# The first layer's feed-forward in the form of the last one: context tokens by themselves, latents as seven block products, the down projection summed in PSUM

## The chip, the cores and the metric

The kernel runs on one core of a Trainium2 chip. The core has a matrix engine (TensorE, PE in the profile; its weight loads are PEld), three engines for elementwise work (VectorE or DVE, ScalarE or ACT, GpSimd or POOL), and SyncE (SP), which here only issues transfers. The engines run side by side, each through a list of instructions of its own, in order, and wait for one another on semaphores. Work tiles lie in SBUF; matmuls write to PSUM, which holds eight banks of 128x512 numbers in fp32. The metric is the device time of one execution in microseconds.

## The reference

A trunk of two layers over a stream of 1024 latent tokens and 256 context tokens, 1024 wide. Each layer mixes the tokens (attention beside a state-space scan, one input and one output projection), and then applies a feed-forward that is 2816 wide. Norms stand ahead of and behind both parts, and a modulation computed from `c` (for the context from `c_ctx`) scales, shifts and gates them. The change is in the feed-forward and its surroundings:

```python
def swiglu(h, w_gate, w_up, w_down):
    return (jax.nn.silu(h @ w_gate) * (h @ w_up)) @ w_down

for l in range(DEPTH):                       # DEPTH = 2
    update_ctx = l < DEPTH - 1
    ...
    f_l = rmsnorm(x_lat, norm_ffn_pre[l]) * (1.0 + sc2_l) + sh2_l
    x_lat = x_lat + g2_l * rmsnorm(swiglu(f_l, w_gate[l], w_up[l], w_down[l]), norm_ffn_post[l])
    if update_ctx:
        ...
        f_c = rmsnorm(x_ctx, norm_ffn_pre[l]) * (1.0 + sc2_c) + sh2_c
        x_ctx = x_ctx + g2_c * rmsnorm(swiglu(f_c, w_gate[l], w_up[l], w_down[l]), norm_ffn_post[l])
return x_lat
```

The first layer's feed-forward works on all 1280 tokens, the last one's on the 1024 latents alone.

## The kernel before

**Tokens and numbers.** The tokens are ten tiles of 128: 0 and 1 are context, 2 to 9 latents. The normed, modulated input of a feed-forward is kept transposed in three buffers: `hc` (context, 256 columns), `ha` (tiles 2 to 5, 512 columns), `hb` (tiles 6 to 9). Each operand in fp32 is split into a high part, a cast on ACT (line 113), and a low part, a subtraction (line 114) on VectorE or POOL. A product is three matmuls, high·high, high·low and low·high, by `mm3` (lines 227 to 229).

**Weights.** A weight *unit* is 512 KB. SP issues its load into one of two buffers `raw`; it is cast and subtracted into one of five ring buffers `w_t`, and `free()` gives the slot to the next unit of a list that `plan()` writes. `pump()` (which `free()` calls) chooses the subtracting engine: POOL for most. A scheduler then orders the instructions on each engine by its own estimate of times; generators (`fill`, `step`) put side work between the steps.

**Feed-forward of layer 0** (`ffn`). The 2816 inner columns are 22 blocks `ff` of 128. It runs twice, first over context and tiles 2 to 5, then over tiles 6 to 9. For each block: gate and up for each span (two PSUM banks `ps_w`, eight steps of `mm3` each), silu on ACT, the product with up (line 1167), a split, and then the down projection of the block, tokens by 1024 columns, in banks `ps_s`. Its result is added on VectorE to `ffn_acc` in SBUF (line 1186; line 1184 copies for the first block). All three weight matrices pass twice: 132 units. Between the blocks run the modulation of the coming layer (`mod_stream`, matmuls of line 278; its 512 KB tiles `raw_m` also go through the two `raw` buffers), the scalings and flips of rows for the next span or layer (`pre_scale` line 361, `pre_flip` line 378), and after the last block `finish`, the norm behind the feed-forward (`postnorm`: squares of line 242, `rstd` lines 234 and 235, lines 806 and 812).

**Feed-forward of layer 1** (`ffn_last`). The latents are a 2x2 block form: two spans of tokens by two halves of the 1024 input columns, blocks B11, B12, B21, B22. For each `ff`, gate and up together are the other factor, with blocks A11, A12 (gate) and A21, A22 (up). Seven block products in place of eight, each four steps of `mm3` over 512 columns, give both results; VectorE adds and subtracts them (for example line 1046). Their factors are A11, A12, A22 and sums S1 to S4 of weight blocks (`wblock`), and B11, B21, B22 and sums T1 to T4 of input blocks, made by `quads` (transposes line 989, sums line 1003, splits lines 998 and 999). Since the sums need the last tiles, three *heads* (the two products A11·B11 and A12·B21) run first. The split result `hid` goes to memory. `down_all` reads it back through `hid_ring` and sums all 22 blocks in PSUM, for groups of tiles (2,3,4), (5,6,7), (8,9), each tile two banks; the down weights pass once per group.

Of the kernel before, what the change touches and what calls it, by code (L numbers as in the profile page):

```python
# [54 lines left out]
class Trunk:  # L55
    def __init__(self, nc, tc, es, I, out):
# [36 lines left out]
        self.hf_d = d("hf", [KT // 2, 2, P, 512])  # L93
        self.hid_d = d("hid", [NFF, P, 2, LAT])
# [34 lines left out]
    def plan(self):  # L129
        I = self.I  # L130
        seq = []
# [13 lines left out]
        for l in range(DEPTH):  # L145
# [8 lines left out]
            if l == 1:  # L154
                flat = [(ff, b) for ff in range(3) for b in ("A11", "A12")]
                flat += [(ff, b) for ff in range(3) for b in (("S4",) if ff == 0 else ()) + ("S2", "S3", "S1", "A22") + (("S4",) if ff else ())]
                flat += [(ff, b) for ff in range(3, NFF) for b in ("A11", "A12", "S2", "S3", "S1", "A22", "S4")]
                self.wpos = {b: (i // 2, i % 2) for i, b in enumerate(flat)}
                for i in range(0, len(flat), 2):
                    seq.append(((l, "w", i // 2), flat[i:i + 2], None))  # L160
                for grp in range(len(self.GROUPS)):
                    for ff in range(NFF):
                        seq.append(((l, "d", grp, ff), [(slice(0, 1024), I["w_down"][l][ff * P:(ff + 1) * P, :].unsqueeze(1))], (1, 1024)))
                break
            for grp in range(2):
                order = [("g", 0), ("u", 0), ("d", 0)]
                for ff in range(1, NFF):
                    order += [("g", ff), ("u", ff), ("d", ff)]
                for kind, ff in order:
                    if kind == "d":  # L170
                        seq.append(((l, kind, grp, ff), [(slice(0, 1024), I["w_down"][l][ff * P:(ff + 1) * P, :].unsqueeze(1))], (1, 1024)))
                    else:
                        w = I["w_gate" if kind == "g" else "w_up"][l]
                        seq.append(((l, kind, grp, ff), [(slice(0, P), kp(w, ff * P, (ff + 1) * P))], (KT, P)))
        self.seq, self.nemit, self.freed, self.U, self.ws = seq, 0, set(), {}, {}

    def pump(self):
        while self.nemit < len(self.seq):
# [11 lines left out]
            self.U[key] = self.unit(parts, shape, None, None if key[1] == "z" or i < 4 or key[2:] == (0, 0) or len(key) == 4 and key[:3] == (1, "d", 2) and key[3] % 2 else self.nc.gpsimd)  # L190
# [7 lines left out]
    GROUPS = ((2, 3, 4), (5, 6, 7), (8, 9))  # L198

    def wblock(self, w, ff, name):  # L200
        nc = self.nc
        st = self.ws.setdefault(ff, {})

        def raw(kind):
            if kind not in st:
                st[kind] = self.raw.tile([P, 1024], F32, tag="raw", name="raw_t")
                src = self.I["w_gate" if kind == "g" else "w_up"][1][:, ff * P:(ff + 1) * P].rearrange("(k p) n -> p k n", p=P)
                nc.sync.dma_start(st[kind].rearrange("p (k n) -> p k n", k=KT), src)
            return st[kind]
# [11 lines left out]
        self.split(w[:, 0], w[:, 1], src, nc.gpsimd)  # L221
        if name == ("A22" if ff == 0 else "S4") or name == "A12" and ff < 3:
# [71 lines left out]
    def mod_stream(self, l, secs, ps):  # L294
        for sec in secs:
# [62 lines left out]
    def pre_scale(self, xs):  # L358
        for a in xs:
            r = self.row_rstd([a[:, 0:512], a[:, 512:1024]], D)  # L360
            self.nc.gpsimd.tensor_scalar(a, a, r, 1.0, op0=ALU.mult, op1=ALU.mult)

    def pre_flip(self, xs, span, i, l, which, keep=None):
# [1012 lines left out]
```

## Time and profile before

Three runs took 3284.16, 3285.5 and 3300.47 us, a median of 3285.5. The profiled execution took 3276.44 us, its span (first to last instruction) is 3274.6 us.

| | |
|---|---|
| Profiled execution; span | 3276.44 us; 3274.6 us |
| Mean granted TensorE clock | 0.975 |
| Layer 0's feed-forward, first to last of its matmuls | 840.15 to 1858.40 us |
| Layer 1's products without a hole | 2640 to 3000 us |
| Layer 1's down projection, some of it | 3040 to 3270 us |

A row of a group of instructions gives line, engine, operation, written and read tiles, shape and count, then busy time and the mean of one in ns, then the idle time of the engine just ahead of them and what ended it. A row of a wait gives who waited for whom, then the total in us, the number of times and the longest. A row of a timeline gives the start and duration in us; an x2 there stands for two instructions in a row. In rows of windows each engine has its busy time and count. The time of one matmul in a timeline includes the depth of the pipeline; the distance between starts is what it costs.

### The profile page before, as it was taken

What the parts mean: (1) busy time and instruction counts of PE and PEld (TensorE: products, weight loads), DVE (VectorE), ACT (ScalarE), POOL (GpSimd) and SP (SyncE); (2) the same over time, 40 slices, a digit from 0 to 9 for tenths busy, and PEclk for the clock granted to TensorE, in tenths of its full rate; (3) what the DMA queues carried; (4) which work ended last, traced back from release to release, by engine and by line L of the source; (5) the groups of instructions that cost most, each with busy time, mean ns of one, the idle gap of its engine ahead of it and who ended that gap; (6) DMA issues with size and microseconds to landing.
All of it is one profiled execution on the core that took longest, in us unless ns stands there. A gap on an engine that the chain in (4) does not pass through costs nothing. (4 is left out here: it accounts for less than half of the span.)

```text
span 3274.6 us, 44714 instructions
## 1 busy us (share of the span) xinstructions
PE 3087.7 (94%) x16411; PEld 2558.0 (78%) x16411; DVE 1725.6 (53%) x3190; ACT 1337.0 (41%) x2441; POOL 1557.2 (48%) x1428
## 2 busy tenths in 40 slices
PE   6999889999899999988999999899999699999997
PEld 4777778888777888876777788688888588888885
DVE  2657567765343344436333556769666665654003
ACT  4433357666422112234222344337666533333232
POOL 4236565444433222336334533755444754454653
PEclk8999899999999999999999999999999899999999
DMA  6376553221333321235444415653222433336776
GB/s 226 100 218 219 188 183 103 65 65 65 116 117 104 99 88 59 71 117 167 135 137 134 136 47 158 223 178 104 65 65 79 134 127 106 110 109 207 240 240 205
DMA packets 328267, 434.61 MB, mean 133 GB/s; under 512 B 22440, under 2 KB 237640, under 8 KB 327792
## 3 DMA queue, kind: packets, MB, share of 16 engines
q1 hardware_dynamic: 268160, 341.04, 33.8%
q10 hardware_dynamic: 59888, 90.71, 7.6%
q8 instruction: 130, 2.13, 0.3%
q14 instruction: 89, 0.73, 0.1%
HBM read 340.67 MB, written 91.01 MB: 132 GB/s over the span
## 5 line engine op out<-in xcount | busy, mean ns | idle before, releaser
L114 POOL TENSOR_TENSOR w_t<-raw_t,w_t 128x1024 fp32r<-128x1024 f32 (+2 forms) x353 | 719.1, 2045 | 1020.2 <-ACT w_t L113 1004.6
L113 ACT CAST w_t<-raw_t 128x1024 fp32r<-128x1024 f32 (+2 forms) x380 | 335.1, 891 | 710.4 <-DMA raw_t<-in_w_down 216.5
L1186 DVE TENSOR_TENSOR ffn_acc<-ffn_acc,ps_s 128x512 f32<-128x512 f32 x400 | 270.9, 686 | 199.9 <-PE ps_s L229 198.4
L862 DVE TENSOR_SCALAR_CACHE_REDUCE att_a<-ps_s 128x512 f32<-128x512 f32 (+1 forms) x400 | 227.1, 587 | 136.8 <-PE ps_s L861 128.5
L870 POOL TENSOR_SCALAR att_a<-att_a,att_st 128x1280 f32<-128x1280 f32 (+1 forms) x144 | 183.2, 1275 | 151.0 <-DVE att_st L869 84.2
L1167 DVE TENSOR_TENSOR s2t<-s2t,ps_w 128x256 f32<-128x256 f32 (+1 forms) x66 | 39.5, 598 | 339.6 <-PE ps_w L229 331.7
L227 PE MATMUL ps_w<-ha,w_t 128*128 128x512 f32 x528 | 208.2, 396 | 6.5 <-DVE s2t L1046 5.5
L228 PE MATMUL ps_w<-ha,w_t 128*128 128x512 f32 x528 | 207.9, 394 | 2.5 <-DVE ha L386 2.5
L229 PE MATMUL ps_w<-ha,w_t 128*128 128x512 f32 x528 | 207.2, 393 | 0.0
L113 ACT CAST xt<-s2t 128x512 fp32r<-128x512 f32 (+2 forms) x147 | 79.9, 543 | 299.1 <-DVE s2t L1167 202.9
L883 PE MATMUL ps_w<-cst_all,att_a 128*128 128x128 f32 x1312 | 197.3, 275 | 0.2
L868 ACT ACTIVATE att_a<-att_a,att_st 128x1280 f32<-128x1280 f32 (+1 forms) x144 | 183.2, 1273 | 33.6 <-DVE att_st L867 30.4
L227 PE MATMUL ps_s<-w_t,xt 128*128 128x512 f32 x446 | 179.9, 403 | 10.2 <-ACT xt L113 4.8
L229 PE MATMUL ps_s<-w_t,xt 128*128 128x512 f32 x446 | 174.9, 395 | 1.5 <-DVE xt L114 1.5
L228 PE MATMUL ps_s<-w_t,xt 128*128 128x512 f32 x446 | 175.7, 394 | 0.0
L114 DVE TENSOR_TENSOR xt<-s2t,xt 128x512 fp32r<-128x512 f32 (+2 forms) x147 | 143.5, 977 | 43.1 <-ACT xt L113 41.6
L883 PEld LDWEIGHTS ps_w<-cst_all,att_a 128*128 128x128 f32 x1312 | 152.8, 141 | 11.0 <-DVE xt L806 5.5
L464 DVE SCALAR_TENSOR_TENSOR xt<-row,convw,xt 128x512 f32<-128x512 f32 (+1 forms) x128 | 123.3, 1017 | 70.0 <-ACT xt L462 52.4
L227 PE MATMUL ps_w<-hb,w_t 128*128 128x512 f32 x352 | 142.3, 404 | 1.1 <-ACT s2t L381 1.1
L228 PE MATMUL ps_w<-hb,w_t 128*128 128x512 f32 x352 | 141.1, 401 | 0.0
L229 PE MATMUL ps_w<-hb,w_t 128*128 128x512 f32 x352 | 140.5, 399 | 0.0
L227 PEld LDWEIGHTS ps_w<-ha,w_t 128*128 128x128 f32 x528 | 100.6, 191 | 28.2 <-DVE s2t L1046 5.7
(355 smaller groups left out, 8405.8 us busy)
## 6 DMA issues: line engine op xcount, KB each, us to landing
raw_t<-in_w_down SPq DMA_DIRECT2D x110, 512.0 KB
raw_m<-in_w_mod SPq DMA_DIRECT2D x80, 512.0 KB
raw_t<-in_w_gate SPq DMA_DIRECT2D x69, 512.0 KB
raw_t<-in_w_up SPq DMA_DIRECT2D x66, 512.0 KB
hid<-xt ACTq DMA_DIRECT2D x44, 512.0 KB
xt<-xs SPq DMA_DIRECT2D x42, 512.0 KB
raw_t<-in_w_in SPq DMA_DIRECT2D x32, 512.0 KB
hid_ring<-hid SPq DMA_DIRECT2D x41, 384.0 KB
```

Of the source, the lines that this page charges most:

```text
L113: self.nc.scalar.copy(hi, src)
L114: (eng or self.nc.vector).tensor_tensor(lo, src, hi.bitcast(F32), op=ALU.subtract)
L227: mm(out, st[0], mv[0], start=first, stop=False)
L228: mm(out, st[0], mv[1], start=False, stop=False)
L229: mm(out, st[1], mv[0], start=False, stop=last)
L464: nc.vector.scalar_tensor_tensor(acc, row[:, o0 + k:o0 + k + n], cw[:, ct, k:k + 1], acc, op0=ALU.mult, op1=ALU.add)
L862: nc.vector.tensor_scalar(pb[:, j:j + m], s[:, :m], -0.125, None, op0=ALU.mult, op1=ALU.min, accum_out=st[:, n:n + 1])
L868: nc.scalar.activation(pb, pb, AF.Exp, bias=nmx, scale=-1.0, accum_out=st[:, 4:5])
L870: nc.gpsimd.tensor_scalar(pb, pb, st[:, 5:6], 1.0, op0=ALU.mult, op1=ALU.mult)
L883: nc.tensor.transpose(tp[:, (2 * k + h) * P:(2 * k + h + 1) * P], pr[h][:, (k2 + k) * P:(k2 + k + 1) * P], self.ident)
L1167: nc.vector.tensor_tensor(s, s, ps["u"][:, :n], op=ALU.mult)
L1186: nc.vector.tensor_tensor(acc[t][:, s], acc[t][:, s], p, op=ALU.add)
```

## The change

The feed-forward of layer 0 takes the form of layer 1's. `ctx_gateup` computes gate and up of the context alone for the 22 blocks (44 units, each with 8 steps over 256 columns) and writes that part of `hid` to memory; the subtraction of up units is on VectorE, that of gate units on POOL. Meanwhile a generator `fill_c` flips tiles 4 and 5, loads tiles 6 to 9 in half rows and makes the sums T1 to T4 by `quads`. B22 can't be kept in `hc`, which the context holds; it goes to a scratch tensor `b22_d`, and `back22` loads and splits it after the context. `ffn` then does the seven products for both layers, with no heads in layer 0. The coming layer's modulation runs at three points of each block; its tiles are now fetched into `x()` buffers one step ahead (`mod_stream(..., ahead)`). `down_all` serves both layers; in layer 0 its groups are tiles (0,1,2,3), (4,5,6), (7,8,9), the first with all eight banks. The norm behind it reads PSUM, and the flips for the next layer are spread over the second and third group. `finish`, the accumulation and the second reading of gate and up go.

In layer 1 there are four heads in place of three, the first `quads` comes ahead of the first head, tiles 6 and 7 are loaded in half rows a stage earlier and scaled there, tiles 8 and 9 are scaled after the first head, the low parts of B22 and T3 are subtracted on VectorE in place of POOL, and so are those of the heads' A11 and A12 and of block 0.

```diff
-            self.U[key] = self.unit(parts, shape, None, None if key[1] == "z" or i < 4 or ...
+            self.U[key] = self.unit(parts, shape, None, None if key[1] in "zu" or i < 4 or ...
...
-    GROUPS = ((2, 3, 4), (5, 6, 7), (8, 9))
+    GROUPS = (((0, 1, 2, 3), (4, 5, 6), (7, 8, 9)), ((2, 3, 4), (5, 6, 7), (8, 9)))
+    HEADS = (0, 4)
...
-        self.split(w[:, 0], w[:, 1], src, nc.gpsimd)
-        if name == ("A22" if ff == 0 else "S4") or name == "A12" and ff < 3:
+        self.split(w[:, 0], w[:, 1], src, nc.vector if head and (ff == 0 or name in ("A11", "A12")) else nc.gpsimd)
+        if name == ("A22" if head and ff == 0 else "S4") or name == "A12" and head:
             st.clear()
...
+        def fetch(i):
+            if i < len(items):
+                got[i] = self.x() if ahead else self.raw.tile([P, 1024], F32, tag="raw", name="raw_m")
+                self.nc.sync.dma_start(got[i], self.mod_src(l, *items[i]))
...
             def tiles(kt):
-                r = self.raw.tile([P, 1024], F32, tag="raw", name="raw_m")
-                self.nc.sync.dma_start(r, self.mod_src(l, sec, kt))
-                return r
+                i = n * KT + kt
+                fetch(i + 1 if ahead else i)
+                return got.pop(i)
...
-            put("B22", b22, nc.gpsimd)
+            if l:
+                put("B22", b22, nc.vector)
+            else:
+                keep = self.s2()
+                nc.gpsimd.tensor_scalar(keep, b22, 1.0, 1.0, op0=ALU.mult, op1=ALU.mult)
+                nc.scalar.dma_start(self.b22_d[k2 // 2, i], keep)
...
-            put("T3", b12, nc.gpsimd)
+            put("T3", b12, nc.vector)
...
+    def back22(self, B):
+        d = B["B22"] = self.block22()
+        for k2 in range(0, 4, 2):
+            for i in range(2):
+                b = self.s2()
+                self.nc.sync.dma_start(b, self.b22_d[k2 // 2, i])
+                v = d[:, k2:k2 + 2, :, 256 * i:256 * i + 256]
+                self.split(v[:, :, 0], v[:, :, 1], b.rearrange("p (k n) -> p k n", k=2))
+
+    def ctx_gateup(self, l, fill):
+        nc = self.nc
+        h = self.hT["hc"]
+        for ff in range(NFF):
+            ps = {}
+            for kind in "gu":
+                u = self.U[l, kind, 0, ff]
+                p = ps[kind] = self.psw()[:, 0:CTX]
+                for kt in range(KT):
+                    self.mm3(p, (u[:, 0, kt], u[:, 1, kt]), (h[:, kt, 0, :], h[:, kt, 1, :]), kt == 0, kt == KT - 1)
+                self.free(l, kind, 0, ff)
+            s = self.s2(n=CTX)
+            nc.scalar.activation(s, ps["g"], AF.Silu)
+            nc.vector.tensor_tensor(s, s, ps["u"], op=ALU.mult)
+            hd = self.x(F32R, n=2 * CTX).rearrange("p (s n) -> p s n", s=2)
+            self.split(hd[:, 0], hd[:, 1], s)
+            nc.scalar.dma_start(self.hid_d[l][ff, :, :, 0:CTX], hd.bitcast(F32))
+            next(fill, None)
...
-        head(0)
-        self.quads(xs0, 0, B)
-        head(1)
-        self.quads(xs1, 1, B)
-        head(2)
-        third(0)
+        heads = self.HEADS[l]
+        if heads:
+            for _ in self.quads(l, xs0, 0, B):
+                pass
+            head(0)
+            self.pre_scale(xs1)
+            head(1)
+            for _ in self.quads(l, xs1, 1, B):
+                pass
+            head(2)
+            head(3)
+            third(0)
...
-                banks = [[self.psw(), self.psw()] if i < 2 else [self.pss(), self.pss()] for i in range(len(ts))]
+                banks = [[a(), b()] for a, b in ((self.psw, self.psw), (self.psw, self.psw), (self.pss, self.pss), (self.psw, self.pss))[:len(ts)]]
...
+            if g:
+                fill()
...
+                    def fill_c():
+                        fl[2]()
+                        yield
+                        xs = [k.row_halves(t, 0) for t in (6, 7)]
+                        B.update(k.blocks(accp))
+                        yield
                         for i in range(2):
...
+                            k.pre_scale(xs)
+                            yield
+                            for _ in k.quads(0, xs, i, B):
                                 yield
...
+                    k.ctx_gateup(0, fc)
+                    drain(fc)
+                    k.back22(B)
...
+                    hx, load = k.ffn(0, B, step(fs), accp)
...
+                    k.down_all(0, hx, load, flip, done)
```

Two places show how the instructions move. On SP, at the start of layer 0's feed-forward, the transfers before are whole rows (`xt<-xs_95`), gate, up and down units and modulation tiles through the same buffers:

```order
L966 DMA xt<-xs_95 128x1024 x2
L124 DMA raw_t<-in_w_gate 128x8x128
L298 DMA raw_m<-in_w_mod 128x1024 x2
L124 DMA raw_t<-in_w_up 128x8x128
L124 DMA raw_t<-in_w_down 128x1024
L124 DMA raw_t<-in_w_gate 128x8x128
```

With the change gate and up units follow one another there, with half rows between them (`s2t<-xs_95`) and the first two blocks' part of the flipped rows (`xt<-hf_117`):

```order
L125 DMA raw_t<-in_w_up 128x8x128
L376 DMA s2t<-xs_95 128x512
L125 DMA raw_t<-in_w_gate 128x8x128
L376 DMA s2t<-xs_95 128x512 x2
L125 DMA raw_t<-in_w_up 128x8x128
L376 DMA s2t<-xs_95 128x512
L125 DMA raw_t<-in_w_gate 128x8x128
L125 DMA raw_t<-in_w_up 128x8x128
L1005 DMA xt<-hf_117 128x512 x2
```

No modulation tile and no down unit is left between them. On POOL, at the opening of layer 1's feed-forward, there stand before three `rstd` and scalings of whole rows in one piece (lines 235 and 361), a weight's subtraction, and the subtractions of `quads` (line 999; `h_hc` is B22, `h_t` are T3 and T4):

```order
L235 TENSOR_TENSOR rstd_t<-rstd_t,mhalf 128x1 x3
L361 TENSOR_SCALAR xt<-xt,rstd_t 128x1024 x3
L114 TENSOR_TENSOR w_t<-raw_t,w_t 128x512
L999 TENSOR_TENSOR h_hc<-xt,h_hc 128x2x256
L999 TENSOR_TENSOR h_t_22918<-xt,h_t_22918 128x2x256
L999 TENSOR_TENSOR h_hc<-xt,h_hc 128x2x256
L999 TENSOR_TENSOR h_t_22918<-xt,h_t_22918 128x2x256
L114 TENSOR_TENSOR w_t<-s2t,w_t 128x512
L114 TENSOR_TENSOR w_t<-raw_t,w_t 128x512
```

With the change the rows' scaling (now line 371) and the flips (line 405) stand there, two subtractions of `quads` (line 1022, T4 alone), and then weights:

```order
L371 TENSOR_SCALAR xt<-xt,rstd_t 128x1024
L405 TENSOR_SCALAR ha<-s2t 128x2x256 x3
L241 TENSOR_TENSOR ss_t<-ss_t 128x1
L231 TENSOR_SCALAR rstd_t<-ss_t 128x1
L232 TENSOR_TENSOR rstd_t<-rstd_t,mhalf 128x1
L371 TENSOR_SCALAR xt<-xt,rstd_t 128x1024
L405 TENSOR_SCALAR ha<-s2t 128x2x256
L1022 TENSOR_TENSOR h_t_22815<-xt,h_t_22815 128x2x256 x2
L115 TENSOR_TENSOR w_t<-s2t,w_t 128x512
L115 TENSOR_TENSOR w_t<-raw_t,w_t 128x512 x3
```

The subtractions for B22 and T3 have left POOL's list for VectorE's.

More of the change, by code (lines that the diff above doesn't have):

```diff
@@ new lines, in blocks, with block22 @@
+    def blocks(self, accp):
+        hb = self.big.tile([P, 8192], F32R, tag="hb", name="h_hb")
+        four = self.four
+        t34 = [accp.tile([P, 4096], F32R, tag=f"t{i}", name=f"h_t{i}") for i in (3, 4)]
+        return {"B11": self.hT["ha"][:, 0:4], "B21": self.hT["ha"][:, 4:8], "T1": four(hb[:, 0:4096]), "T2": four(hb[:, 4096:8192]),
+                "T3": four(t34[0]), "T4": four(t34[1])}
+    def block22(self):
+        return self.four(self.big.tile([P, 4096], F32R, tag="hc", name="h_hc"))
@@ L1039, in head @@
         def head(ff):
-            x1, sa = [accp.tile([P, 512], F32, name=f"head{i}") if ff == 2 else self.s2() for i in range(2)]
+            if ff == 3:
+                g = self.grp.tile([P, D], F32, tag="grow", name="head_g")
+                x1, sa = g[:, 0:512], g[:, 512:1024]
+            else:
+                x1, sa = [accp.tile([P, 512], F32, name=f"head{i}") if ff == 2 else self.s2() for i in range(2)]
             a = self.psw()
@@ L1072, in rest @@
             emit_hid(sa, ff, 0)
[L1073 to L1074 removed]
+            if "x3" in st:
+                p = st.pop("x3")
             else:
@@ L1136, in down_all @@
                 if ff == NFF - 1:
-                    self.finish_psum(l, t, banks[i])
+                    done(t, self.finish_psum(l, t, banks[i]))
             self.free(l, "d", g, ff)
-            load(n + 9)
+            load(n + ahead)
+            if g:
+                fill()
     def finish_psum(self, l, t, halves):
-        if self.fgrow[0] != (l, 0):
-            self.fgrow = ((l, 0), self.gate_row(l, 5, "norm_ffn_post", 0))
-        self.postnorm(halves, self.x(), t, self.fgrow[1], 2 * l, self.out[0, (t - NCT) * P:(t - NCT + 1) * P, :], t % 2 == 0, t == NT - 1)
@@ L1301, in fill_a @@
                         for i in range(2):
[L1302 removed]
+                            k.pre_scale(xs)
+                            yield
+                            for _ in k.quads(0, xs, i, B):
                                 yield
[L1304 to L1312 removed]
@@ L1355, with flip @@
+                    def flip():
+                        while todo and next(todo[0], todo) is todo:
+                            todo.pop(0)
+                    k.down_all(0, hx, load, flip, done)
+                    late = [lambda: drain(todo.pop(0))] * len(todo)
+                else:
+                    B = k.blocks(accp)
+                    B["B22"] = k.block22()
+                    k.down_all(1, *k.ffn(1, B, lambda: None, accp, fl[2], [k.last_x[t] for t in (8, 9)]))
 NAMES = ["x", "c", "ctx", "c_ctx", "w_mod", "b_mod", "norm_mix_pre", "norm_mix_post", "norm_ffn_pre", "norm_ffn_post",
```

281 lines of the change are left out of this document (109 added, 172 removed).

## The prediction

> **What bounds the kernel now.** The page's first part comes first, then its group of VectorE additions that the change deletes.
>
> ```profile
> PE 3087.7 (94%) x16411; PEld 2558.0 (78%) x16411; DVE 1725.6 (53%) x3190; ACT 1337.0 (41%) x2441; POOL 1557.2 (48%) x1428
> L1186 DVE TENSOR_TENSOR ffn_acc<-ffn_acc,ps_s 128x512 f32<-128x512 f32 x400 | 270.9, 686 | 199.9 <-PE ps_s L229 198.4
> ```
>
> TensorE sets the time; no other engine passes 53%. The 270.9 us of accumulation lie beside it, so deleting them is worth only what TensorE waited for them. What counts is the number of matmuls and the holes between them. The stages by windows (length; busy time of each engine; granted clock; DMA share; GB/s):
>
> ```profile
> core 0: us, PE busy (x) PEld busy (x) DVE busy (x) ACT busy (x) POOL busy (x), PEclk, DMA share, GB/s
> 840.15:1858.40 1018.25, 983.05 (x5034) 794.15 (x5034) 434.62 (x595) 267.57 (x419) 380.76 (x243) 0.98 0.36 112
> 2535.16:2612.00 76.84, 52.09 (x206) 41.02 (x207) 48.58 (x46) 45.71 (x98) 61.06 (x62) 0.80 0.47 151
> 2640.00:3000.00 360.00, 360.00 (x1576) 295.44 (x1575) 209.29 (x281) 129.87 (x225) 179.31 (x129) 1.00 0.36 116
> 3040.00:3160.00 120.00, 120.00 (x531) 99.38 (x530) 5.36 (x7) 34.70 (x42) 77.61 (x40) 1.00 0.74 250
> 3200.00:3270.00 70.00, 53.43 (x222) 40.30 (x220) 21.44 (x18) 20.57 (x25) 24.16 (x16) 0.97 0.58 196
> ```
>
> In order: layer-0 feed-forward, opening of layer 1's, its seven products, its three-tile down groups, its last two-tile group. The layer-0 row has 1018.25 − 983.05 = 35.2 us of idle, and a clock of 0.98, another 0.02 × 1018 = 20 us: 56 us lost. The form that the change brings runs without a hole in layer 1, products and three-tile groups alike; there 120.00 / 531 = 0.226 us is a 512-column matmul. Its two weak places are the opening (24.8 us idle, clock 0.80) and the last group (16.6 idle). Who is waited for in the layer-0 window:
>
> ```profile
> PE ps_w L278 <- DMA raw_m<-in_w_mod: 18.2, 7, 6.5
> PE ps_s L227 <- ACT xt L113: 4.8, 3, 1.9
> PE ps_w L378 <- POOL xt L361: 3.1, 2, 2.5
> PE ps_s L227 <- DVE ffn_acc L1186: 2.9, 3, 1.5
> PE ps_s L227 <- ACT ffn_acc L1184: 2.5, 1, 2.5
> ```
>
> Half is the modulation matmul waiting for its tile, which shares two `raw` buffers with the weights. The accumulation itself holds TensorE for 5.4 us.
>
> **The change part by part.** *Matmuls.* Latent gate and up were 22 blocks × 2 matrices × 8 × 2 spans × 3 = 2112 matmuls of 512 columns; seven products of 4 × 3 are 22 × 84 = 1848. Context (1056 of 256 columns), down (1320) and modulation stay. So 264 × 0.226 = **−59.7 us**, all on TensorE.
>
> *Modulation tiles* now go to `xt` buffers, one step ahead. In the products 56 tiles over 22 × 84 × 0.226 = 418 us give each about 7 us, the longest wait above being 6.5. They pass the weights on SP's queue, in a stage that moved 116 GB/s where 250 is shown without a hole. I take the 18.2 us as gone; 0 to 5 may come back, if an `xt` buffer is late because a `hid` write still reads it.
>
> *Context stage (new).* 1056 matmuls of 256 columns:
>
> ```profile
> 43.85 0.28 PE L227 MATMUL ps_s<-hc,w_t 128*128 128x256 f32 x1
> 44.09 0.28 PE L229 MATMUL ps_s<-hc,w_t 128*128 128x256 f32 x1
> 48.42 0.80 PE L227 MATMUL ps_s<-hc,w_t 128*128 128x256 f32 x2 [4.04 <-POOL hc L385]
> 50.77 0.41 PE L228 MATMUL ps_s<-hc,w_t 128*128 128x256 f32 x1
> 50.99 0.41 PE L229 MATMUL ps_s<-hc,w_t 128*128 128x256 f32 x1
> ```
>
> The first two are two matmuls apart, 0.24 / 2 = 0.12 us each: 127 us, and some 5 us of transposes, 132 in all. One gate and one up unit feed only 48 × 0.12 = 5.8 us of matmuls. Before, the same pair also fed 512 latent columns (48 × 0.226 = 10.8 more) and one down unit; now weights can set the pace. Gate units are subtracted on POOL, up units on VectorE. The nearest row is the last group of layer 1, where pairs of units go through the same two buffers with the same division:
>
> ```profile
> PE ps_w L228 <- POOL w_t L114: 8.0, 7, 1.3
> 3221.51 2.36 POOL L114 TENSOR_TENSOR w_t<-raw_t,w_t 128x1024 fp32r<-128x1024 f32 x1 [4.53 <-ACT w_t L113]
> 3256.60 2.37 POOL L114 TENSOR_TENSOR w_t<-raw_t,w_t 128x1024 fp32r<-128x1024 f32 x1 [4.56 <-ACT w_t L113]
> ```
>
> Six of POOL's subtractions, first and last shown, are (3256.60 − 3221.51) / 5 = 7.02 us apart: one pair per 7.02 us. The start is in these rows:
>
> ```profile
> 829.25 2.35 DVE L114 TENSOR_TENSOR w_t<-raw_t,w_t 128x1024 fp32r<-128x1024 f32 x2
> 840.15 0.58 PE L227 MATMUL ps_w<-hc,w_t 128*128 128x256 f32 x1
> ```
>
> The first pair is split at 831.6, before TensorE begins at 840.15; the second stands at about 838. The last of 22 is then ready at 838 + 20 × 7.02 = 978 and used by 984; TensorE alone would end at 840 + 132 = 972. I take **14 us lost** here; at 6.4 us a pair it is 0, at 9 us 52.
>
> *Seam to the products.* The latent tiles' quarters and context sums are made on VectorE, POOL and ACT while TensorE does the context, the fourth quarter goes to memory and comes back after the stage. In the opening of layer 1 the same work holds TensorE; here it has 140 us of cover. Left over: the load and split of the fourth quarter, used only by the first block's last product. I take 4 us, and 3 at the stage's start.
>
> *Down groups.* The first has four tiles and takes all eight banks, so the next group's first matmul waits for a bank to be emptied, on this chain:
>
> ```profile
> L242 ACT ACTIVATE junk<-ps_w 128x512 f32<-128x512 f32 x48 | 28.7, 598 | 76.0 <-PE ps_w L229 75.4
> L235 POOL TENSOR_TENSOR rstd_t<-rstd_t,mhalf 128x1 f32<-128x1 f32 x92 | 55.5, 605 | 6.6
> L806 DVE SCALAR_TENSOR_TENSOR xt<-ps_w,rstd_t,gate_row 128x512 f32<-128x512 f32 x48 | 33.7, 746 | 135.4 <-POOL rstd_t L235 135.3
> L812 POOL TENSOR_TENSOR xt<-xt 128x1024 f32<-128x1024 f32 x20 | 48.6, 2428 | 23.5 <-DVE xt L806 23.4
> ```
>
> Two squares 1.2, rstd 0.6, one 0.75 and what is issued between them: some 3 us for the first tile, whose matmuls end three tiles (18 matmuls, 4 us) ahead of the last. Behind POOL's 2.4 us addition or a weight's subtraction the later tiles slip: **4 us** (bounds 0 and 8). Queued behind that waiting matmul is only its own group; the ring refills meanwhile. In groups two and three POOL has the weights, ten tiles' scalings and flips, against 77.61 of 120 us in the three-tile row: 5 us (0 to 15). With 5 for the clock the stage loses 14 + 4 + 3 + 4 + 5 + 5 ≈ 35 where it lost 56: **−21 us**. The rate rises: 1018 × 112 = 114 MB before, 22 more down units (11.5 MB) and `hid` out and back (2 × 22 × 128 × 2 × 1280 × 4 bytes = 58 MB) make 183 MB in some 940 us, 195 GB/s, under the 250 shown.
>
> *Opening of layer 1.* What holds TensorE there, and the prices:
>
> ```profile
> PE ps_w L989 <- POOL xt L361: 8.3, 2, 8.0
> PE ps_w L227 <- DVE s2t L1046: 5.5, 1, 5.5
> PE ps_w L378 <- POOL xt L361: 3.7, 1, 3.7
> PE ps_w L228 <- DVE ha L386: 2.5, 1, 2.5
> L999 POOL TENSOR_TENSOR h_t<-xt,h_t 128x512 fp32r<-128x512 f32 x7 | 11.8, 1688 | 2.0 <-ACT h_t L998 2.0
> L999 DVE TENSOR_TENSOR h_hb<-xt,h_hb 128x512 fp32r<-128x512 f32 x7 | 10.5, 1524 | 0.0
> L114 POOL TENSOR_TENSOR w_t<-raw_t,w_t 128x512 fp32r<-128x512 f32 x14 | 19.1, 1378 | 2.7 <-ACT w_t L113 2.7
> ```
>
> The late rows (8.0) are now scaled a stage earlier, and a fourth head brings 24 × 0.226 = 5.4 us of products forward. Against it: 8 subtractions of the quarters (8 × 1.52 = 12.2) and 13 of the heads (about 0.69 each, half of POOL's price: 9.0) move to VectorE, whose 48.6 us become some 70 of a stage of 77. VectorE is then what ends late. 76.8 + 5.4 − 70 leaves 12; I take **−8**. Bounds: the four waits above sum to 19.7, so −20; if 20 us of VectorE's waits stay beside its 70, 90 − 82 = +8.
>
> *Sum:* −59.7 − 21 − 8 = −89. On the profiled execution: 3276.4 − 89 = 3188; the median of the runs is 9 us higher, 3285.5 − 89 = 3196. I say **3194**.
>
> **The rivals.**
>
> *Slower context pairs.* If POOL's copies of the fourth quarter, the scalings and sums get between the subtractions, a pair takes 9 us: 38 us more than at 14 lost, **3233**. For: POOL's order is fixed in the listing, and a 2.4 us operation ahead delays a buffer. Against: only four such batches lie in 22 pairs.
>
> *The holes close.* A pair at 6.4 us, no bank wait, no loss in the groups (−14 − 4 − 5) and an opening at −20 (12 more): 3194 − 35 = **3159**. For: products and three-tile groups in layer 1 are without a hole.
>
> *The buffers serialise; the other side.* ACT's casts stand in one queue with the silu that waits for the pair's own matmuls. If the second buffer's cast waits for those, the two buffers no longer overlap and a pair takes 2 × 7.02 = 14 us: +140, **3334**, slower. It decides from about 12.5 us a pair (107 us above the forecast). For: casts did wait on TensorE before.
>
> ```profile
> L113 ACT CAST w_t<-raw_t 128x1024 fp32r<-128x1024 f32 x240 | 251.6, 1050 | 591.9 <-DMA raw_t<-in_w_down 216.5 <-PE ps_s L229 119.3 <-PE ps_w L229 83.5
> ```
>
> Against: the ring of five holds two more pairs, and the last group keeps 7.02.
>
> *Half clock in the context stage.* After the pause of 4.04 us at 48.42 the 256-column matmuls came 0.22 us apart, not 0.12. If the stage's pauses keep it there, a pair takes 48 × 0.22 = 10.6 us, 22 × 3.5 = +78: **3272**, no measurable change. Against: its pauses are 7.02 − 5.8 = 1.2 us, and the last group, idle 24% of its time in pauses of at most 1.3, kept 0.97. The Trainium skill, "TensorE: Matmul & The Clock Gate", section "HAM oscillation — how this bites in real kernels", gives the point from which this happens as idle gaps above about 3.4 us; by that rule pauses of 1.2 leave the clock alone, and the trace agrees on both sides, 4.04 and 1.3.
>
> That the change does not do what it says is excluded: the matmul counts follow from the order.
>
> **How the numbers follow.** Forecast 0.57, slower pairs 0.16, holes closed 0.17, serialised 0.05, half clock 0.05. A difference of 0.5%, 16 us, is about what a measurement of this kernel tells from none: faster is the first three, 0.90; same 0.05; slower 0.05. Range 3150 to 3240 takes in the first three cases; the forecast's own is 3168 to 3218.
>
> **What would show it.** Right: about 0.226 us a matmul without holes in the layer-0 products; no wait of L278's successor on `in_w_mod`; context subtractions on POOL about 7 us apart, 130 to 150 us from the first context matmul to the products; a wait of some 4 us for a bank after the first down group; VectorE the releaser in layer 1's opening. Wrong: waits on `w_t` inside the products, a clock under 0.9 in the context stage, waits on `hid_ring`, or a time above 3269, which only a stage that the profile of before does not show could make.

## The result, and the profile after

Four runs of the changed kernel took 3234.5 to 3241.5 us, a median of **3236.1**, against 3284.8 for the kernel before in the same session: a ratio of **0.9833** with a 95% interval of 0.9812 to 0.9853. It is faster by 1.7%, 49 us where 91 were forecast. The time lies in the range (3150 to 3240), near its upper end, but outside the forecast's own (3168 to 3218) and next to the rival of slower context pairs (3233). The profiled execution took 3234.5 us, its span 3232.7, 41.9 less than before.

TensorE still sets the time. The page's first part, and the changed kernel by stages in the columns used before (context stage, products, down projection; then layer 1's opening, products, three-tile groups and last group):

```profile
PE 3041.5 (94%) x16147; PEld 2517.7 (78%) x16147; DVE 1665.7 (52%) x3093; ACT 1410.9 (44%) x2595; POOL 1663.6 (51%) x1529
```

```profile
855.60:1030.55 174.95, 146.94 (x1105) 142.69 (x1105) 81.76 (x99) 86.21 (x152) 84.06 (x66) 0.93 0.67 207
1030.55:1503.40 472.85, 470.47 (x2299) 352.21 (x2298) 257.88 (x346) 155.55 (x271) 216.92 (x163) 1.00 0.51 174
1503.40:1832.40 329.00, 315.83 (x1369) 254.40 (x1368) 33.62 (x33) 101.89 (x152) 200.10 (x131) 0.98 0.65 215
2525.30:2605.00 79.70, 69.95 (x299) 56.08 (x298) 65.72 (x85) 47.25 (x94) 38.00 (x33) 0.89 0.36 113
2630.00:2950.00 320.00, 320.00 (x1401) 262.71 (x1400) 194.54 (x256) 116.51 (x205) 165.23 (x119) 1.00 0.35 115
2990.00:3130.00 140.00, 140.00 (x619) 115.99 (x618) 5.27 (x7) 39.99 (x47) 88.00 (x45) 1.00 0.72 244
3150.00:3220.00 70.00, 60.66 (x256) 47.08 (x256) 21.22 (x17) 21.44 (x27) 28.13 (x19) 1.00 0.70 240
```

The products of layer 0 run nearly without a hole, 470.47 us busy of 472.85. The context stage and the down projection do not. Who TensorE waits for between the first context matmul and the last down matmul:

```profile
PE ps_w L224 <- ACT w_t L114: 19.2, 12, 3.4
PE ps_w L398 <- POOL xt L371: 13.9, 2, 8.3
PE ps_s L225 <- POOL w_t L115: 1.9, 1, 1.9
PE ps_w L226 <- DVE w_t L115: 1.9, 2, 1.1
```

It waits for casts of weights, and for two flips whose rows are not yet scaled. The waits for modulation tiles and for the accumulation are gone. From the starts of the first and last matmuls of each stage, the 41.9 us come together like this:

| from … to | before | after | difference | forecast |
|---|---|---|---|---|
| start … first context matmul of layer 0's feed-forward | 840.15 | 855.60 | **+15.4** | 0 |
| … last down matmul of it | 1017.9 | 976.6 | −41.3 | −81 |
| … last matmul of layer 1's out projection | 688.0 | 693.1 | +5.1 | 0 |
| … last product of layer 1 | 463.5 | 444.8 | −18.7 | −8 |
| … end | 265.1 | 262.7 | −2.4 | 0 |

So 39 us of the forecast are missing in layer 0's feed-forward, and 15 were lost ahead of it, in a part of the program where each engine's list of instructions is the same in both kernels. Most of that loss is one instruction. POOL's timeline, before and then after, in the convolution stage of layer 0:

```profile
125.23 1.47 POOL L114 TENSOR_TENSOR w_t<-raw_t,w_t 128x528 fp32r<-128x528 f32 x1 [3.60 <-ACT w_t L113]
```

```profile
125.19 13.01 POOL L115 TENSOR_TENSOR w_t<-raw_t,w_t 128x528 fp32r<-128x528 f32 x1 [3.60 <-ACT w_t L114]
```

The same subtraction, started at the same time within 0.04 us, lasts 13.01 us in place of 1.47. SP's next modulation tile waits for the buffer, and TensorE for the tile:

```profile
PE ps_w L275 <- DMA raw_m<-in_w_mod: 9.1, 1, 9.1
```

The stage's first matmul with swapped operands comes 11.3 us later (204.0 for 192.7).

### The profile page after: what moved, and what is told of

Read it like the earlier page. It is cut to its first block, busy times and chain, and to the rows that moved or that the text cites. A ratio compares the mean times of both kernels' runs of the same rounds, so it can differ in the third digit from the quotient of the medians.

```text
span 3232.7 us, 44982 instructions
## 1 busy us (share of the span) xinstructions
PE 3041.5 (94%) x16147; PEld 2517.7 (78%) x16147; DVE 1665.7 (52%) x3093; ACT 1410.9 (44%) x2595; POOL 1663.6 (51%) x1529
## 4 chain that ended last, share of the span: by engine, by line
PE 73%; DMA 9%; DVE 6%; POOL 5%; ACT 3%; issue 3%; SPq 0%; ACTq 0%; DVEq 0%; POOLq 0%
PE ps_w L224 11%; PE ps_w L225 11%; PE ps_w L226 11%; PE ps_s L224 7%; PE ps_s L225 7%; PE ps_s L226 7%; PE ps_w L912 5%; PE ps_w L905 4%; PE ps_s L883 4%; POOL w_t L115 3%; DMA raw_t<-in_w_down 2%; DMA raw_t<-in_w_up 2%; ACT w_t L114 1%; PE ps_w L275 1%; PE ps_w L755 1%
## 5 line engine op out<-in xcount | busy, mean ns | idle before, releaser
L115 POOL TENSOR_TENSOR w_t<-raw_t,w_t 128x512 fp32r<-128x512 f32 (+2 forms) x430 | 795.7, 1861 | 834.3 <-ACT w_t L114 806.1
L114 ACT CAST w_t<-raw_t 128x512 fp32r<-128x512 f32 (+2 forms) x490 | 389.3, 810 | 774.4 <-PE ps_s L226 240.5
L225 PE MATMUL ps_w<-w_t,hid_ring 128*128 128x512 f32 x523 | 207.5, 397 | 8.6 <-POOL w_t L115 8.6
L226 PE MATMUL ps_w<-w_t,hid_ring 128*128 128x512 f32 x523 | 206.3, 395 | 0.0
L224 PE MATMUL ps_w<-w_t,hid_ring 128*128 128x512 f32 x523 | 195.9, 395 | 3.7 <-ACT w_t L114 3.1
L828 DVE SCALAR_TENSOR_TENSOR xt<-ps_w,rstd_t,gate_row 128x512 f32<-128x512 f32 x57 | 40.0, 746 | 230.8 <-POOL rstd_t L232 168.8
L115 DVE TENSOR_TENSOR w_t<-raw_t,w_t 128x1024 fp32r<-128x1024 f32 (+1 forms) x60 | 69.9, 1173 | 168.9 <-ACT w_t L114 168.9
L115 DVE TENSOR_TENSOR xt<-s2t,xt 128x512 fp32r<-128x512 f32 (+2 forms) x144 | 121.7, 846 | 48.2 <-ACT xt L114 46.6
L224 PE MATMUL ps_w<-ha,w_t 128*128 128x512 f32 x352 | 138.5, 394 | 2.3 <-ACT xt L1016 2.3
L225 PE MATMUL ps_w<-ha,w_t 128*128 128x512 f32 x352 | 138.8, 394 | 2.0 <-DVE ha L406 2.0
L226 PE MATMUL ps_w<-ha,w_t 128*128 128x512 f32 x352 | 138.2, 393 | 0.0
L225 PEld LDWEIGHTS ps_w<-w_t,hid_ring 128*128 128x128 f32 x523 | 98.9, 189 | 34.0 <-POOL w_t L115 12.0
L224 PE MATMUL ps_w<-hc,w_t 128*128 128x256 f32 x352 | 106.1, 302 | 19.6 <-ACT w_t L114 17.6
L224 PEld LDWEIGHTS ps_w<-w_t,hid_ring 128*128 128x128 f32 x523 | 98.7, 189 | 26.8 <-ACT w_t L114 4.0
L226 PEld LDWEIGHTS ps_w<-w_t,hid_ring 128*128 128x128 f32 x523 | 98.9, 189 | 21.4
```

The source lines that it names most:

```text
L114: self.nc.scalar.copy(hi, src)
L115: (eng or self.nc.vector).tensor_tensor(lo, src, hi.bitcast(F32), op=ALU.subtract)
L224: mm(out, st[0], mv[0], start=first, stop=False)
L225: mm(out, st[0], mv[1], start=False, stop=False)
L226: mm(out, st[1], mv[0], start=False, stop=last)
```

## The experiments

Single runs differ by chance in that early stall, so they are compared by the length of a stage. Among the runs that leave a part as it is, the context stage took 171.4 to 174.9 us, the products 471.3 to 474.1, the down projection 327.6 to 334.6, the part from there to the last matmul of layer 1's out projection 691.2 to 697.8, and from that matmul to layer 1's last product 444.3 to 446.6. The changed kernel's own context stage, 174.9, is the longest of its group, so a gain against it is stated as a range.

**1. The early stall.**

```diff
-None if key[1] in "zu" or ...
+None if key[1] in ("z", "u", "kv") or ...
```

> The change, with the four 128x528 weight subtractions per layer that stand in the convolution stage moved from POOL to VectorE; nothing else moves. Theory: in the changed kernel POOL's 13.01 us for one such subtraction at 125.19 us (1.47 us before the change) is a wait for VectorE's unbroken row of convolution steps, and it delays everything behind it by 11.3 us; the same happens in layer 1 in both kernels (13.03 us). Then no such stall is left, the first context matmul comes at about 844 us in place of 855.6, and the time falls by 15 to 22 us, to about 3212 to 3220. Rival: the delay is a late modulation tile, whatever POOL does: the first context matmul stays at 855 and the time at 3230 to 3240.

The stall is gone, and VectorE takes 0.7 us for such a subtraction. The first context matmul, after the change and in this run:

```profile
855.60 0.58 PE L224 MATMUL ps_w<-hc,w_t 128*128 128x256 f32 x1
```

```profile
129.26 0.69 DVE L115 TENSOR_TENSOR w_t<-raw_t,w_t 128x528 fp32r<-128x528 f32 x1
844.60 0.58 PE L224 MATMUL ps_w<-hc,w_t 128*128 128x256 f32 x1
```

The matmul comes 11.0 us earlier, and the profiled span is 3220.0, 12.7 shorter, where 15 to 22 were expected. The median is 3226.4 us (3221.8 to 3236.1), ratio 0.9813 with 0.9776 to 0.9851: that interval overlaps the change's own, so the gain is shown by the trace and not by the times. The rival, a late tile whatever POOL does, is refuted. In layer 1 the stall went too and gained nothing that shows: from the last down matmul to the out projection it takes 693.3 us here and 693.1 with the stall.

The other runs tell more, since the stage's instructions are the same in nearly all of them. Each layer has four such subtractions, and only the first ever stalls. Of the twelve traces with it on POOL, nine have the 13 us stall in layer 0 (the changed kernel and e2, e3, e5 to e10), three don't (the kernel before, e4, e11), and all twelve have it in layer 1. Here is e4, in which it failed to appear in layer 0:

```profile
126.11 1.48 POOL L115 TENSOR_TENSOR w_t<-raw_t,w_t 128x528 fp32r<-128x528 f32 x1 [3.60 <-ACT w_t L114]
```

In each of the 21 stalls 16 instructions of VectorE's convolution steps end, without a gap between them, while POOL waits, and POOL ends 1.15 to 1.19 us after the last. In the changed kernel that row of steps is

```profile
116.90 20.13 DVE L485 SCALAR_TENSOR_TENSOR xt<-row,convw,xt 128x770 f32<-128x770 f32 x23
```

which ends at 137.03, and POOL's subtraction at 138.20. Where POOL got through, one VectorE instruction beside it took 1.81 us in place of 0.74 (before, at 125.44). The two exclude each other. What decides which of them gets in stays open: in all 24 cases POOL's subtraction began 0.71 to 0.73 us after a VectorE instruction of about 1.0 us, whether it then stalled or not. The Trainium skill, "SBUF — State Buffer", section "Who interferes with whom", says that a VectorE instruction with two SBUF inputs contends with a GpSimd instruction that reads SBUF, that the port pair they share is an exclusive lock, and that the order of issue decides who blocks. The trace agrees on the exclusion; but the one that came later waited for 16 instructions, not one, and in three of 24 cases it did not wait.

**2. The context stage: the form of the loads.** The context's part of layer 0's feed-forward is then computed from other weights, so this run serves for its times alone.

```diff
-[(slice(0, P), kp(w, ff * P, (ff + 1) * P))]
+[(slice(0, P), I["w_down"][l][ff * P:(ff + 1) * P, :].rearrange("p (k n) -> p k n", k=KT))]
```

> The change, with the context stage's 44 units read from whole rows of the down weights (4 KB pieces) in place of column blocks of gate and up (512-byte pieces); the order on PE, VectorE, ACT and POOL is the same, and the feed-forward of layer 0 is computed from the wrong weights for the context. Theory: the column blocks land about 0.7 us later (3.9 against 3.2 us), and that makes a pair of units 7.7 us in place of the 7.02 of the forecast: POOL's subtractions late in the stage are then 7.0 us apart and the context stage takes about 162 us in place of 175. Rival: POOL and ACT are held by the block sums and their copies: 7.7 us and 175 us stay.

The stage took 164.1 us in place of 174.9, or 7 to 11 us less than in the runs with column blocks. POOL's subtractions of gate units late in the stage, the first and last of ten after the change, then here:

```profile
952.51 2.35 POOL L115 TENSOR_TENSOR w_t<-raw_t,w_t 128x1024 fp32r<-128x1024 f32 x1 [2.86 <-ACT w_t L114]
1021.67 2.40 POOL L115 TENSOR_TENSOR w_t<-raw_t,w_t 128x1024 fp32r<-128x1024 f32 x1 [5.57 <-ACT w_t L114]
```

```profile
952.87 2.42 POOL L115 TENSOR_TENSOR w_t<-raw_t,w_t 128x1024 fp32r<-128x1024 f32 x1 [2.27 <-PE ps_w L226]
1014.91 2.40 POOL L115 TENSOR_TENSOR w_t<-raw_t,w_t 128x1024 fp32r<-128x1024 f32 x1 [4.41 <-ACT w_t L114]
```

That is (1021.67 − 952.51) / 9 = 7.68 us a pair, and (1014.91 − 952.87) / 9 = 6.89. The forecast's 7.02 came from units read in whole rows; gate and up units are column blocks and take longer: most gate units late in the stage are cast 3.8 to 4.3 us after their issue, the same units in whole rows 3.2 to 3.7. The first half of the stage changed little: pairs there were about 9 us apart in both.

**3. The round of a buffer.**

```diff
-None if key[1] in "zu" or ...
+None if key[1] in "zug" or ...
```

> The change, with the gate units of the context stage subtracted on VectorE like the up units. Theory (each buffer's round of load, cast and subtraction sets the pace): 2.36 becomes 1.23 us, a pair takes 6.4 to 6.7 us and the context stage 150 to 158 us. Rival (the memory's rate sets it): 7.7 us a pair and 172 to 176 us stay.

The stage took 159.1 us, with 6.75 us a pair in the second half (945.1 to 999.1 us, eight pairs); both lie just above what was expected. A subtraction shortened by 1.13 us shortens the pair by 0.9, so the rate of memory alone does not set it.

**4. The flip that the second block waits for.**

```diff
                     def fill_c():
+                        yield
+                        yield
                         fl[2]()
```

> The change, with the flip of tiles 4 and 5, on which the second context block waits 5.6 us, and everything behind it in that generator two blocks later. Theory A: the wait was uncovered time, and the context stage is 5 to 6 us shorter (169 us). Theory B: weights set the pace of the whole stage, and since the ring fills during the wait, the wait costs nothing or little: 173 to 177 us.

The wait for the flip is gone, and the stage took 176.0 us: no gain. The wait of 5.6 us in the changed kernel costs nothing where weights set the pace.

**5. A flip in the down projection.**

```diff
-todo.append(k.flip_steps(xs, *pairs[t], 1, 0))
+todo.append(itertools.chain([None] * (3 if t == 5 else 0), k.flip_steps(xs, *pairs[t], 1, 0)))
```

> The change, with the flip of tiles 4 and 5 for the next layer begun three steps later in the third down group. Theory: TensorE's 8.3 us wait there is a flip that stands in its list ahead of the tile's norm (squares, rstd, addition, scaling); three steps of 4.1 us cover it, and the down projection takes 319 to 322 us in place of 328.8. Rival: the flips only move behind the last down matmul, where nothing covers them: the down projection is shorter, but the first matmul of layer 1 comes no earlier (within 2 us).

The down projection took 319.5 us in place of 328.8. The wait that it removes, in the changed kernel:

```profile
1739.64 0.47 PE L398 MATMUL ps_w<-cst_all,xt 128*128 128x128 f32 x1 [8.28 <-POOL xt L371]
```

The rival is refuted by its own sign: layer 1's first matmul starts 0.24 us after the last down matmul, here as in the changed kernel, so it comes earlier by the whole gain. From there to layer 1's out projection 698.0 us follow, against 693.1 in the changed kernel and up to 697.8 in runs that leave that part as it is, so it is not shown that any of the gain is given back there. The two parts together are 1017.5 us, against 1021.9 in the changed kernel and 1021.1 to 1029.1 in the runs that leave both as they are.

**6. Layer 1's opening: the work moved to VectorE.**

```diff
-            if l:
-                put("B22", b22, nc.vector)
+            if l:
+                put("B22", b22, nc.gpsimd)
...
-            put("T3", b12, nc.vector)
+            put("T3", b12, nc.gpsimd if l else nc.vector)
...
-self.split(w[:, 0], w[:, 1], src, nc.vector if head and (ff == 0 or name in ("A11", "A12")) else nc.gpsimd)
+self.split(w[:, 0], w[:, 1], src, nc.gpsimd)
```

> The change, with layer 1's low parts of B22 and T3 and the heads' weight subtractions back on POOL; four heads and the earlier rows stay. From the last matmul of layer 1's out projection to the last product it takes 444.8 us with the change and 463.5 before. Theory A (VectorE is the late one, as the forecast said, and the move is a small loss or nothing): 440 to 446. Theory B (POOL was the late one, and the move is what shortened the opening): 451 to 460.

From the out projection to the last product it takes 458.5 us, 13.7 more than with the change. Theory B holds; the move to VectorE is most of the gain.

**7. Layer 1's opening: the order.**

```diff
-    HEADS = (0, 4)
+    HEADS = (0, 3)
...
+            self.pre_scale(xs1)
+            head(0)
             for _ in self.quads(l, xs0, 0, B):
                 pass
-            head(0)
-            self.pre_scale(xs1)
             head(1)
...
-            head(3)
...
-                        if l:
-                            fl[2] = [k.row_halves(t, 2) for t in (6, 7)]
...
+                        else:
+                            fl[2] = k.pre_load(SB, 0, 2)
+                            k.pre_scale(fl[2])
```

> The change, with layer 1's opening in the order of before (three heads, first sums after the first head, rows loaded whole and scaled at the last stage of attention, last rows scaled ahead of the first head); the moves to VectorE stay. Theory A (order and early rows are what shortened the opening): 455 to 463 us from the out projection to the last product in place of 444.8, and 5 us less ahead of it (attention's end with 688 in place of 693 us from the last down matmul). Theory B (the moves to VectorE did it): 445 to 450.

The same part takes 452.8 us, 8.0 more, and between the theories: 13.7 + 8.0 = 21.7 is about the 18.7 gained. The 5 us ahead of it did not come back (696.2 us): order and early rows are not what lengthened that part.

**8. A third load buffer.**

```diff
-        self.raw = pool("raw", bufs=2)
+        self.raw = pool("raw", bufs=3)
...
-        self.s2p = pool("s2", bufs=8)
+        self.s2p = pool("s2", bufs=6)
```

> The change, with three load buffers for weights in place of two (and six in place of eight small work tiles, to make room). Theory (a buffer's round of load, cast and subtraction sets the context stage's pace): three buffers bring a pair of units to about 5 us, under TensorE's 5.8, and the stage to 135 to 148 us in place of 175. Rival (the memory's rate, or ACT's order, sets it): 165 to 175 us.

The context stage took 154.4 us, less than any run with two buffers but more than the 135 to 148 expected; the last part, from the last product to the end, 249.8 us in place of 262.7. In the stage's second half pairs are now 5.7 us apart, which is TensorE's own pace:

```profile
952.59 2.39 POOL L115 TENSOR_TENSOR w_t<-raw_t,w_t 128x1024 fp32r<-128x1024 f32 x1 [2.55 <-ACT w_t L114]
975.48 2.40 POOL L115 TENSOR_TENSOR w_t<-raw_t,w_t 128x1024 fp32r<-128x1024 f32 x1 [3.30 <-DVE w_t L115]
```

These are four intervals, (975.48 − 952.59) / 4 = 5.72 us. What remains is the first half. The flip's wait is there as with two buffers (6.0 us), and new waits beside it: TensorE waits for rows that are not yet scaled, and for a bank that ACT has yet to empty.

```profile
PE ps_w L1012 <- POOL s2t L371: 4.8, 3, 3.9
PE ps_w L1012 <- ACT xt L1016: 3.3, 1, 3.3
```

Layer 1 pays for it: from its out projection to its last product it takes 450.4 us, 4 to 6 more than in the runs that leave that part alone. Whether the third load buffer or the two missing work tiles cost this was not tried.

**9. Modulation tiles through the weights' buffers.**

```diff
-yield from k.mod_stream(0, (5,), k.psw, True)
+yield from k.mod_stream(0, (5,), k.psw)
```

and so for the other three calls.

> The change, with the modulation tiles in layer 0's products fetched as before the change: into the weights' two load buffers, at the step that uses them. Theory A (the forecast's: sharing two buffers made the 18.2 us of waits): TensorE waits again for these tiles, 10 us or more, and the products take 483 to 500 us in place of 472.9. Theory B (the products need only one weight unit per 9.5 us, so the buffers have room): 472 to 477 us.

The edit takes away both the buffers of their own and the fetch one step ahead. The products took 600.1 us, 127 more, and the time was 3358 us. Both theories are wrong on the size. In the products of this run TensorE waits for the weights more than for the tiles:

```profile
PE ps_s L224 <- ACT w_t L114: 53.1, 7, 9.7
PE ps_w L275 <- DMA raw_m<-in_w_mod: 30.2, 12, 4.9
```

A block's gate and up halves stay in the two buffers until all seven factors are made from them, so a third tenant holds up both. The 53.1 us are a price of the sharing; how much of the 30.2 is owed to the late fetch was not told apart. The block products cannot well share these two buffers.

**10. The block sums after the context stage.**

```diff
                         fl[2]()
-                        yield
+                        for _ in range(NFF):
+                            yield
                         xs = [k.row_halves(t, 0) for t in (6, 7)]
```

> The change, with the loading of tiles 6 to 9 and all block sums left until the context stage is over. Theory (their transfers and ACT's share of them are what makes the pairs of the stage's first half 8.9 us long, against 7.4 in its second half): pairs are 7.2 to 7.7 us throughout and the context stage takes 155 to 162 us in place of 175; the sums then stand uncovered for 45 to 80 us before the products. Rival: the first half's pairs stay near 8.9 us without the sums, and the stage at 170 us or more.

The stage took 161.7 us, with even pairs: the first and last of 13 subtractions are

```profile
916.90 2.38 POOL L115 TENSOR_TENSOR w_t<-raw_t,w_t 128x1024 fp32r<-128x1024 f32 x1 [5.00 <-ACT w_t L114]
1006.19 2.38 POOL L115 TENSOR_TENSOR w_t<-raw_t,w_t 128x1024 fp32r<-128x1024 f32 x1 [4.91 <-ACT w_t L114]
```

That is (1006.19 − 916.90) / 12 = 7.44 us. The sums then hold TensorE: from the last context matmul to the first down matmul it takes 513.0 us, 40 more than with the change. So the loads and sums cost 10 to 13 us beside the context and 40 behind it, a little under the 45 expected.

**11. The place of the read-back buffers.**

```diff
-            elif l:
+            elif False:
...
-        ahead = 9 if l else 8
+        ahead = 8
```

> The change, with layer 1's read-back buffers for the hidden blocks placed like layer 0's (in the room of the sums T3 and T4, in two rings of four). In layer 0's down groups the matmuls start 0.233 us apart on average, in layer 1's 0.2265. Theory A (the place of these buffers sets it): layer 1's three-tile groups go to 0.230 to 0.235. Theory B (something else in layer 0): they stay at 0.2265.

In layer 1's three-tile groups the median distance between starts of matmuls went from 227 ns to 232 (mean 226.7 to 232.4), as in layer 0 of the changed kernel (mean 232.8 where nothing is waited for). Theory A holds: the place of the tiles from which `hid` is loaded as weights costs 5.7 ns a matmul. The edit also loads eight blocks ahead in place of nine, but TensorE waits for none of them in either run. What about the place does it was not tried.

**12. Three of them together.** The edits of 1, 5 and 8.

> The change, with three load buffers, the convolution stage's weight subtractions on VectorE and the later flip in the third down group, together. If the three act each by itself as measured alone (about 30, 8 to 11 and 4 us of span), the time is 3186 to 3196; if the later flip and the third buffer answer for the same wait, 3192 to 3202.

The median is **3192.8 us** (3189.1 to 3201.6), ratio to the kernel before **0.9717**, interval 0.9682 to 0.9753, wholly below the change's own. It beats both kernels. The median lies in both of the expected ranges, so the time does not choose between the theories. The stages do: the down projection took 315.3 us, 13.4 less than with the change, where the later flip alone gave 9.3 and the third buffer 3.1, so in that stage the two add up, as far as the spread of single runs allows to say. Layer 1 again gives some of it back: 701.7 us up to the end of its out projection and 450.4 to its last product, both longer than in the runs named at the head of this section. The stages of its feed-forward of layer 0 (context, products, down):

```profile
842.00:996.10 154.10, 140.01 (x1105) 138.10 (x1104) 102.70 (x103) 86.05 (x155) 85.04 (x69) 0.94 0.76 230
996.10:1470.00 473.90, 469.83 (x2300) 352.40 (x2299) 263.11 (x343) 153.99 (x269) 214.53 (x162) 1.00 0.51 173
1470.10:1785.50 315.40, 312.87 (x1369) 252.79 (x1368) 40.29 (x33) 101.89 (x152) 200.81 (x130) 1.00 0.68 224
```

## Why the prediction was right and where it was wrong

**Right: the matmuls.** The page counts 16147 where it counted 16411, the 264 less that were worth −59.7 us. The products took 472.8 us: 1848 × 0.2265 make 418.6 of it, and the 448 modulation matmuls take most of the rest; waits are 2.3.

**Right: the modulation tiles, and more than forecast.** No wait on them is left in the feed-forward. What was valued at 18.2 us would cost 127 in the new form, as the ninth run showed for buffers and early fetch together.

**Wrong: "The last of 22 is then ready at 838 + 20 × 7.02 = 978".** The stage's 14 and 3 us of loss were 174.9 − 132 = 43. (The prediction's own figures, 984 and 972, leave 12, not 14.) Two terms failed. The price of a pair came from units read in whole rows; column blocks load slower, and whole rows give 7 to 11 us back. And the pace was taken as one for the whole stage, where the block sums and their loads make its first half slower; without them the stage is 10 to 13 us shorter. The rival "slower context pairs" had the result right, 9 us a pair there, but its mechanism wrong. Not POOL's queue delayed the subtractions: in 20 of 21 cases POOL began within 0.13 us of the end of a gate unit's cast. It was the stretch from a gate unit's issue to its cast, mostly 3.8 to 4.3 us late in the stage and up to 7.0 in its first half. The changed kernel's trace tells what lengthens it there, in ACT's idle time ahead of these casts. The first row is from the first half, and without a bracket, so no idle time stood ahead of it; the second row is from the second half:

```profile
880.38 1.09 ACT L114 CAST w_t<-raw_t 128x1024 fp32r<-128x1024 f32 x1
951.39 1.05 ACT L114 CAST w_t<-raw_t 128x1024 fp32r<-128x1024 f32 x1 [4.70 <-DMA raw_t<-in_w_gate]
```

Of nine gate casts from 869 to 944 us, six began without idle time, straight behind other work in ACT's list. Of the ten after that, each had 1.6 to 4.7 us of idle time ahead of it, ended in eight by the landing of the unit. So the casts of the first half waited mostly in ACT's list, behind the sums' work, and those of the second half for transfers.

**Wrong: 3 us for the start.** TensorE waits 5.6 us for the flip at the second block; but the fourth run showed that it costs nothing there.

**Too high: the seam to the products and the banks.** The seam cost 0.1 us in place of 4. The wait for a bank behind the first down group, forecast at 4 us, is this row:

```profile
PE ps_w L224 <- DVE xt L828: 0.6, 1, 0.6
```

The first tile's chain of squares, rstd and scaling takes from 1621.3 to 1626.4 us, but the other three tiles' matmuls run until 1625.5 and cover most of it. That is inside the stated bounds (0 to 8), but the middle value was too high.

**Wrong: 5 us "in groups two and three".** The down projection lost 24.5 us against its nominal 304.3 (1320 × 0.2265, and 48 flips at 0.11). Waits for weights are 1.6 + 0.8 + 1.9 = 4.3 of it; the flip that stands ahead of its own norm 8.3, and some 2 more for the ten matmuls behind it, which came 0.43 us apart; the place of the `hid` buffers 1320 × 0.0057 = 7.5. The first two were in the stated bounds (0 to 15), the place in no term.

**Wrong way round: the opening of layer 1.** It gained 18.7 us in place of 8, within the bounds (the four waits that set the lower one sum to 20.0, not 19.7). The step that failed is "VectorE is then what ends late": the prediction counted the move to VectorE as a cost, and undoing it costs 13.7. In the new opening VectorE is busy 65.72 of 79.70 us, near the 70 worked out, but it runs beside 69.95 us of TensorE work; the sum of busy times said nothing about which result was late. The sign that was named came in part: of the 10 us that TensorE waits there, 5.3 are for VectorE and 4.4 for ACT, and none is for POOL. The 5.1 us ahead of the opening were in no term, and their cause stays open; every run in the new form took 691.2 us or more there, where the one trace of before has 688.0. At the end of attention TensorE waits for rows to flip:

```profile
PE ps_w L398 <- POOL xt L371: 3.9, 1, 3.9
```

**Not foreseen: 15.4 us ahead of the stage.** Of these 11.3 are the one stalled subtraction. Without it the first context matmul comes at 842 to 845 us, 2 to 4 after that of before; that rest is unexplained.

**Luck.** That the time fell in the range is in part luck, since errors cancelled: with the 8 us forecast for the opening in place of 18.7 the time would be 3247, above the range; without the stalled subtraction it would be 3225. In neither case would the forecast's own path, a context stage of about 149 us, have been right.

**The rivals.** Serialised buffers (14 us a pair) did not occur. Half clock did not hold over the stage (the granted clock was 0.93), but it occurred in five stretches with 95 of the 1056 matmuls, 0.21 in place of 0.12 us apart: some 9 us at most, of which the pace of the weights covers a part. It began with the stage, and at or soon after waits like these of the changed kernel:

```profile
869.28 1.12 PE L398 MATMUL ps_w<-cst_all,xt 128*128 128x128 f32 x4 [5.63 <-POOL xt L371]
956.64 0.58 PE L224 MATMUL ps_w<-hc,w_t 128*128 128x256 f32 x1 [3.39 <-ACT w_t L114]
1002.34 0.39 PE L224 MATMUL ps_w<-hc,w_t 128*128 128x256 f32 x1 [2.07 <-ACT w_t L114]
```

The prediction took pauses of 1.2 us for all of the stage and let the clock alone; the pauses came uneven. The point of about 3.4 us that the prediction took from the Trainium skill ("TensorE: Matmul & The Clock Gate", section "HAM oscillation — how this bites in real kernels") agrees with the first two rows, not with the third, 1.3 us after which the rate halved as well. A pair of 5.7 to 5.8 us, faster than the fast rival's 6.4, is what a third buffer brings in the second half.

## What to carry to other kernels

A price for a load must come from loads of the same form: here a 512 KB unit in 512-byte pieces took some 0.6 us more than one in whole rows, and in a stage bound by two buffers that was paid pair by pair. When a stage loses the matmuls that covered its side work, count that side work in the round of the load buffers too (on ACT's list here), not only on TensorE. And compare stages, not spans: one instruction, in a stage that most edits leave alone, moved the whole kernel by 11 us in nine of twelve traces, and would have hidden or faked the effect of an edit.

## What the runs showed of the hardware that was not expected

A two-input subtraction on POOL can wait for an unbroken row of 16 two-input VectorE instructions, 13.0 us in place of 1.47. It did so in 21 of 24 cases, each time for the first of a layer's four; the other three began in the same way and got through. With the subtraction on VectorE the wait is gone, at 0.7 us each.

A matmul whose loaded operand is read from another place in SBUF starts 232.4 in place of 226.7 ns after the one ahead of it, with the same list of instructions on TensorE.
